# Moving the on-the-way weight sums of the second layer's output projection from pairs 2 and 3 to pairs 4 and 5, with side work in every second step

## The chip, the cores and the metric

The kernel runs on one core of a Trainium2 chip. The metric is the device time of one execution in microseconds (us). The time before is the median of three runs, 2347.38 us (2345.62 to 2347.71).

## The reference, cut to what matters

One inference step of a two-layer decoder over 1024 prompt tokens and 8 decode tokens, width 2048. Layer A is a pooling mixer, layer B is windowed attention with a gate. Both end in an output projection, a residual and a layer norm. The change touches the output projection of layer B alone:

```python
def attn_layer(x, pos, kb, vb, k_pos, q_pos, blocked, w_in, sinks, w_out, g_ln, b_ln):
    ...
    o = attn_core(q, kb, vb, q_pos, k_pos, sinks).reshape(B, T, D_ATTN)
    y = (o * jax.nn.silu(gate)) @ w_out
    return layer_norm(ALPHA * x + y, g_ln, b_ln)
```

## The kernel before

**Phases.** The tokens are cut into two chunks, chunk 0 with 512 columns and chunk 1 with 520. The phases run one after the other: `ai` (input projection and pooling of layer A), `ao` (its output projection), `bi` (input projection and attention of layer B), `bo` (its output projection). "bo, chunk 0" is the second output projection's first chunk. It follows "bi, chunk 1", and "bo, chunk 1" follows it and ends the kernel.

**Strassen products.** A product of 2048 by 2048 weights is worked in eight pairs of output tiles, here pair 0 to pair 7. Each pair is one 2x2 block product by a seven-product scheme. The four weight blocks of a pair are a11, a12, a21 and a22, each 128 x 1024 fp32 (512 KB). Three of the seven products use a block as it stands (indices 0, 5 and 6: a11, a12, a22). Four use sums of blocks (indices 1 to 4). In f32r every product is made from a high part and a low part, so one product is three matmuls for each of eight slices of K: lines 655, 656 and 657 (high x high, high x low, low weight x high), 24 matmuls in all.

**Steps.** One such product is a step. Bo, chunk 0 has 56 steps, counted here from 0. Pairs 0 and 1 are interleaved in steps 0 to 13 (`both`). Pair p from 2 on has steps 7p to 7p + 6 in the order of indices 0, 2, 1, 5, 3, 4, 6 (`ORDER7`). So pair 2 has steps 14 to 20, pair 3 steps 21 to 27, pair 4 steps 28 to 34, pair 5 steps 35 to 41.

**What a step issues.** `begin` first flushes the evictions of the step before (`posts`: lines 594, 600, 603, 609, 615, 628 on ACT, lines 616 and 621 on DVE, and after a pair's last product line 1234, the residual, on DVE). Then it loads weights, casts them to their high part (line 476, ACT), takes the low part (line 491, DVE), and makes sums. How far ahead each is done stands in `self.ahead`, (a, b, d): at step e weights are loaded up to step e + a - 1, cast up to e + b - 1, and their low part is taken up to e + d - 1. Sums are made up to e + b. From the last pair of bi on, `ahead` is (6, 3, 2). From the end of step 23 of bo, chunk 0 it is (7, 4, 3). The first of the three matmuls that needs the low part is line 657, the third matmul of a step.

**Where the sums come from.** There are two ways. `next_pair` loads all seven blocks ready made, the four sums from the scratch tensor `swob`, into which `sum_gen` has put them during bi (lines 425 to 430). `first_pair` loads the four blocks (a22 twice, five loads), makes the sums on the way with four additions on DVE (line 334), uses them, and stores them to `swob` (line 335, a DMA issued from POOL), since chunk 1 needs them again. `LATE` names the pairs of `wob` that go by `first_pair` in bo, chunk 0. `sum_gen` leaves these out.

**Other work in bo, chunk 0.** After each pair come line 1277 (subtract the shift), 1283 (square, ACT), 1288 and 1289 (two running sums), all 128 x 1024, and a store (line 1279, POOL). In steps 0 to about 20 the last of the attention and the decode tokens' attention still run (lines 1759 to 1979). From step 18 on there is side work, the generator `t_gen` for the activations "o" of chunk 1: a load (line 836, SP), four subtractions and additions of 128 x 260 on DVE (lines 823 to 826) and a store (line 827, POOL), eight times. It advances by one item in `end`, at most once in `self.every` steps:

```python
        if self.side and int(self.i / self.every) != int((self.i - 1) / self.every) and room >= self.room:
            if next(self.side[0], 1):
                self.side.pop(0)
```

`every` is 3 for a phase that does not set it, so also for bo, chunk 0. What is left is done at once when the next phase's inputs are first wanted (`x_begin`, between steps 41 and 42). From there on the activations of chunk 1 are loaded, cast (line 766) and split (line 775) beside the weights.

**Order.** PE, DVE and ACT each run in the order of the source (`in_order`), so an instruction that waits holds all behind it. SP issues the loads and POOL most stores, each in an order that the scheduler sets from the readiness of the buffers. All large tiles share 53 slots (`Mem`).

Of the kernel before, what the change touches and what calls it, by code (L numbers as in the profile page):

```python
# [69 lines left out]
    (7, 3), (7, 4), (5, 5), (5, 6), (6, 5), (6, 6), (7, 5), (7, 6),  # L70
)

LATE = (2, 3)
X_KEEP = 5
X_AGE = 3
SIDE_KEEP = 5
# [106 lines left out]
class Kern:  # L183
# [177 lines left out]
    def build_stream(self):  # L361
        io = self.io
        w = []
        for kind, c, part in PHASES:
# [20 lines left out]
            else:  # L385
                name = "woa" if kind == "ao" else "wob"
                if (kind, c, part) != PHASES[-1]:
                    prs = [self.next_pair(name, q) for q in range(8)]
                    if (kind, c) == ("bo", 0):
                        for q in LATE:  # L390
                            prs[q] = self.first_pair(name, q)
# [10 lines left out]
    def sum_gen(self, name):  # L402


        W = 256
        qs = [q for q in range(8) if name != "wob" or q not in LATE]
        parts = [(q, slice(W * h, W * h + W)) for q in qs for h in range(4)]
# [144 lines left out]
    def both(self, c, P, Q):  # L552

        runs = [self.seven(c, z0, z1, {6: done}, own=own) for (z0, z1, done), own in (
            (P, self.psW), (Q, self.psW if self.wide else self.psO)
        )]
        for idx in ORDERL:
            for run in runs:
                run(idx)

    def pair(self, c, z0, z1, done, c11=None):

        run = self.seven(c, z0, z1, {6: done}, c11)
        for idx in ORDER7:
            run(idx)
# [1535 lines left out]
    def run(self):  # L2101
        io = self.io
        self.build_stream()
        self.needs, self.pe, self.summed, self.hurry = [], {}, {}, None
        self.sg, self.qs, self.ao = {}, {}, {}
        self.last = self.turn = self.lock = False
        self.need = {}
        self.shared = False
        self.strassen = False
        self.start()  # L2110

        def add(key, gen):
            self.needs.append((key, gen))
            self.side.append(gen)

        acc, before = {}, False
        for n, (kind, c, part) in enumerate(PHASES):
            self.c, self.ph = c, kind + str(c)
            self.strassen = (kind, c, part) not in PLAIN
            self.shared = False  # L2120
            self.fresh = c == 1 and before and self.strassen
            before = c == 0 and self.strassen
            nxt = n + 1 if n + 1 < len(PHASES) else None
            self.every, self.room = 3, SIDE_KEEP
            if n == 0 or (kind, c) == ("bi", 0) and self.wide:
                self.use_four(kind == "ai")
            elif (kind, c) == ("bo", 0):
                self.at(18, lambda: self.use_four(True))

            self.lock = (kind, c) in LOCKED  # L2130
            self.need = {
                (idx, g): self.i + (2 * n + g - 1 if self.lock else n)
                for n, idx in enumerate(ORDERL if self.lock else ORDER7) for g in range(2)
            } if self.strassen else {}
            self.turn = not self.lock
            self.at(7, lambda: setattr(self, "turn", False))
            self.at(13, lambda: setattr(self, "lock", False))
            if n == 0:
                pass
            elif (kind, c) == ("ai", 0):  # L2140
                add(("x", 1, False), self.t_gen(("x", 1)))
                self.room = 99
            elif (kind, c) == ("ai", 1):
                add(("g", 0, False), self.t_gen(("g", 0)))
                self.summed["woa"] = 0
                add("woa", self.sum_gen("woa"))
                self.every = 1.7
            elif (kind, c) == ("ao", 0):
                self.every = 2
            elif (kind, c) == ("ao", 1):  # L2150
                gen = self.ln_gen(0, *acc[0], C_GA, C_BA, self.act["h", 0], None)
                self.at(3, lambda gen=gen: add(("h", 0, True), gen))
                self.every = 2
            elif (kind, c) == ("bi", 0) and not self.strassen:
                self.summed["wob"] = 0
                self.extra = self.sum_gen("wob")
                for k in (4, 24):
                    self.at(k, lambda k=k: setattr(self, "on", k == 4))
                add(("h", 1, False), self.ln_gen(1, *acc[1], C_GA, C_BA, self.act["h", 1], self.Td.get(("h", 1))))
                add(("h", 0, False), self.t_gen(("h", 0)))  # L2160

                for k in range(10):
                    self.at(2 * k + 3, lambda: self.side and self.lastO < self.i - 1 and self.side_step())
                self.every = 1.2
            elif (kind, c) == ("bi", 1):
                self.at(8, lambda: setattr(self, "on", True))
                self.every, self.room = 1, 0
            elif (kind, c) == ("bo", 0):
                self.at(23, lambda: setattr(self, "ahead", (7, 4, 3)))
                self.at(18, lambda: add(("o", 1, False), self.t_gen(("o", 1))))  # L2170
                self.at(16, lambda: [s.free() for s in self.kv])
                self.rt.free()
            elif (kind, c) == ("bo", 1):
                gen = self.ln_gen(0, *acc[0], C_GB, C_BB, io["y0"], None)
                self.at(3, lambda gen=gen: add("y", gen))
                self.every = 3
            if kind == "ai":
                self.phase_ai(c, range(*part), nxt)
            elif kind == "bi":
                self.phase_bi(c, range(*part), nxt)  # L2180
            else:
                res = self.act["x" if kind == "ao" else "h", c]
                last = (C_GB, C_BB, io["y1"]) if nxt is None else None
                acc[c] = self.phase_out(c, res, nxt, last)
# [146 lines left out]
```

## Time and profile before

| | us |
|---|---|
| median of three runs | 2347.38 |
| the profiled execution, whole | 2344.57 |
| its span, first to last instruction | 2342.8 |

The profiled execution is 2.81 us under the median. What lies around its span is 1.77 us. In the lines shown below, a row of a timeline has start, duration, engine, line, operation and operands, and in square brackets the idle time before it and what ended it. A row of a list of groups has count, busy time and mean. A row of the windows has the busy time of PE, PE's weight loads, DVE, ACT and POOL in that stretch, then the granted clock, the share of the DMA engines and GB/s. Times in a timeline count from the start of the span.

### The profile page before, as it was taken

What the parts mean: (1) busy time and instruction counts of PE and PEld (TensorE: products, weight loads), DVE (VectorE), ACT (ScalarE), POOL (GpSimd) and SP (SyncE); (2) the same over time, 40 slices, a digit from 0 to 9 for tenths busy, and PEclk for the clock granted to TensorE, in tenths of its full rate; (3) what the DMA queues carried; (4) which work ended last, traced back from release to release, by engine and by line L of the source; (5) the groups of instructions that cost most, each with busy time, mean ns of one, the idle gap of its engine ahead of it and who ended that gap; (6) DMA issues with size and microseconds to landing.
All of it is one profiled execution on the core that took longest, in us unless ns stands there. A gap on an engine that the chain in (4) does not pass through costs nothing. (4 is left out here: it accounts for less than half of the span.)

```text
span 2342.8 us, 49652 instructions
## 1 busy us (share of the span) xinstructions
PE 2302.7 (98%) x19960; PEld 2202.7 (94%) x19960; DVE 1923.7 (82%) x2386; ACT 1365.4 (58%) x2502; POOL 202.3 (9%) x379
## 2 busy tenths in 40 slices
PE   8999999999999999999999999999999999999997
PEld 6899999999999999998777899999999999999997
DVE  8788988777878878868998898897777778889887
ACT  4454446544546557655464666685666668556656
POOL 0111110010000000000111111100000000000000
PEclk9999999999999999999999999999999999999999
DMA  8668789989889989999799766788776768699785
GB/s 293 213 242 310 272 287 343 328 290 326 299 302 328 323 286 329 320 339 325 262 330 360 254 235 225 253 297 279 249 249 231 231 199 299 230 355 371 268 303 196
DMA packets 252072, 669.39 MB, mean 286 GB/s; under 512 B 25760, under 2 KB 106560, under 8 KB 251840
## 3 DMA queue, kind: packets, MB, share of 16 engines
q1 hardware_dynamic: 206368, 501.14, 63.3%
q0 software_dynamic: 45472, 165.07, 18.2%
q8 instruction: 156, 2.56, 0.4%
q14 instruction: 76, 0.62, 0.1%
HBM read 471.01 MB, written 185.59 MB: 280 GB/s over the span
## 5 line engine op out<-in xcount | busy, mean ns | idle before, releaser
L655 PE MATMUL pD<-m,m 128*128 128x260 f32 (+1 forms) x4752 | 1346.2, 283 | 4.7 <-ACT pD L594 2.8
L657 PE MATMUL pD<-m,m 128*128 128x260 f32 (+1 forms) x4752 | 1340.3, 282 | 6.2 <-DVE m L491 6.1
L656 PE MATMUL pD<-m,m 128*128 128x260 f32 (+1 forms) x4752 | 1339.8, 282 | 1.1 <-DVE m L775 1.1
L491 DVE TENSOR_TENSOR m<-m,m 128x1024 fp32r<-128x1024 f32 x674 | 814.2, 1219 | 114.8 <-ACT m L476 59.7
L655 PEld LDWEIGHTS pD<-m,m 128*128 128x128 f32 x4752 | 895.5, 188 | 13.2 <-issue 5.1
L657 PEld LDWEIGHTS pD<-m,m 128*128 128x128 f32 x4752 | 895.9, 189 | 8.5 <-DVE m L491 8.5
L656 PEld LDWEIGHTS pD<-m,m 128*128 128x128 f32 x4752 | 895.5, 188 | 1.8 <-DVE m L775 1.3
L476 ACT CAST m<-m 128x1024 fp32r<-128x1024 f32 x674 | 703.4, 1049 | 251.5 <-DVE m L334 69.6
L683 PE MATMUL pD<-m,m 128*128 128x512 f32 x448 | 179.5, 401 | 8.1 <-ACT m L766 8.1
L684 PE MATMUL pD<-m,m 128*128 128x512 f32 x448 | 177.2, 395 | 1.0 <-DVE m L775 1.0
L685 PE MATMUL pD<-m,m 128*128 128x512 f32 x448 | 177.0, 395 | 0.0
L775 DVE TENSOR_TENSOR m<-m,m 128x1024 fp32r<-128x1024 f32 (+1 forms) x120 | 146.9, 1225 | 6.9 <-ACT m L766 5.4
L766 ACT CAST m<-m 128x1024 fp32r<-128x1024 f32 (+1 forms) x120 | 125.8, 1052 | 14.1 <-PE pD L684 5.2
L683 PEld LDWEIGHTS pD<-m,m 128*128 128x128 f32 x448 | 84.6, 189 | 29.5 <-ACT m L766 8.1
L334 DVE TENSOR_TENSOR m<-m,m 128x1024 f32<-128x1024 f32 x88 | 107.6, 1222 | 4.3 <-DMA m<-in_wia 2.6
L684 PEld LDWEIGHTS pD<-m,m 128*128 128x128 f32 x448 | 84.6, 189 | 20.8 <-DVE m L775 2.1
L685 PEld LDWEIGHTS pD<-m,m 128*128 128x128 f32 x448 | 84.5, 189 | 19.7
L616 DVE TENSOR_TENSOR m<-pD,m 128x260 f32<-128x260 f32 (+1 forms) x86 | 36.0, 419 | 80.6 <-ACT pD L615 73.8
L628 ACT COPY m<-pD 128x260 f32<-128x260 f32 (+1 forms) x83 | 31.0, 374 | 117.9 <-PE pD L657 117.8
L1795 ACT ACTIVATE m<-m,sm 128x128 f32<-128x128 f32 x256 | 99.2, 391 | 0.0
L1085 PE MATMUL pD<-m,m 128*128 128x260 f32 (+1 forms) x528 | 91.5, 323 | 0.0
L1808 ACT ACTIVATE m<-m,sm 128x128 f32<-128x128 f32 x256 | 81.9, 392 | 12.8 <-DVE sm L1803 12.8
(245 smaller groups left out, 2113.1 us busy)
## 6 DMA issues: line engine op xcount, KB each, us to landing
m<-in_wia SPq DMA_DIRECT2D x124, 512.0 KB
m<-in_wib SPq DMA_DIRECT2D x120, 512.0 KB
swia<-m POOLq DMA_DIRECT2D x64, 512.0 KB, 4.8
m<-swia SPq DMA_DIRECT2D x64, 512.0 KB
m<-swoa SPq DMA_DIRECT2D x64, 512.0 KB
swib<-m POOLq DMA_DIRECT2D x64, 512.0 KB, 5.4
m<-swib SPq DMA_DIRECT2D x64, 512.0 KB
m<-swob SPq DMA_DIRECT2D x56, 512.0 KB
```

What stands on the lines that cost most here:

```text
L334: self.nc.vector.tensor_add(s[out].a[:, :1024], s[x].a[:, :1024], s[y].a[:, :1024])
L476: self.nc.scalar.copy(hi.r[:, :1024], self.stream[self.cast].src().a[:, :1024])
L491: self.nc.vector.tensor_sub(lo.r[:, :1024], s.src().a[:, :1024], hi.a[:, :1024])
L655: nc.tensor.matmul(ps[:, :TH], wh[:, s], h, start=new and k == 0, stop=False, skip_group_check=on)
L656: nc.tensor.matmul(ps[:, :TH], wh[:, s], l, start=False, stop=False, skip_group_check=on)
L657: nc.tensor.matmul(ps[:, :TH], wl[:, s], h, start=False, stop=k == 7, skip_group_check=on)
L683: nc.tensor.matmul(ps[:], wh[:, s], h, start=par == 0 and k == 0, stop=False)
L684: nc.tensor.matmul(ps[:], wh[:, s], l, start=False, stop=False)
L685: nc.tensor.matmul(ps[:], wl[:, s], h, start=False, stop=par == 1 and k == 7)
L766: self.nc.scalar.copy(h.r[:, :n], s.a[:, :n])
L775: self.nc.vector.tensor_sub(l.r[:, :n], s.a[:, :n], h.a[:, :n])
L1795: nc.scalar.activation(x["s3"][:, i, :], x["s3"][:, i, :], AF.Exp, bias=nm[:, i : i + 1], scale=0.125, accum_out=rs[:, i : i + 1],)
```

## The change

`LATE` names pairs 4 and 5 in place of pairs 2 and 3, and the phase bo, chunk 0 advances its side work every second step in place of every third.

```diff
-LATE = (2, 3)
+LATE = (4, 5)
@@ run
             elif (kind, c) == ("bo", 0):
+                self.every = 2
                 self.at(23, lambda: setattr(self, "ahead", (7, 4, 3)))
                 self.at(18, lambda: add(("o", 1, False), self.t_gen(("o", 1))))
```

Both programs have the same number of instructions on PE, DVE, ACT and POOL. `sum_gen` makes the sums of pairs 0, 1, 2, 3, 6 and 7 during bi in place of 0, 1, 4, 5, 6 and 7. On DVE the eight additions of line 334 and the eight groups of lines 823 to 826 stand elsewhere. On POOL and SP the stores and loads that belong to them move along.

## The prediction

> **What bounds the kernel now.** I read the page's first part, then PE's waits, then the timelines of PE, DVE and ACT over bo, chunk 0.
>
> ```profile
> PE 2302.7 (98%) x19960; PEld 2202.7 (94%) x19960; DVE 1923.7 (82%) x2386; ACT 1365.4 (58%) x2502; POOL 202.3 (9%) x379
> ```
>
> PE is busy 2302.7 of 2342.8 us, so everything the change can win is in PE's idle time, and what it can lose is new idle time. The change reaches only bo, chunk 0 and what follows. PE's waits between 2010 and 2060 us, the steps in which pairs 2 and 3 make their sums, are these (total, times, longest):
>
> ```profile
> PE pD L657 <- DVE m L491: 2.5, 4, 1.4
> PE pS L1836 <- DVE m L1822: 0.7, 1, 0.7
> ```
>
> All five wait for DVE, four for the low part of a weight. Those that matter here, with the start of step 21 (2047.82) and of step 22 (2050.61), and one in the next activations' stage:
>
> ```profile
> 2025.77 1.97 PE L1836 MATMUL pS<-m,m 128*64 128x128 f32 x32 [0.70 <-DVE m L1822]
> ...
> 2028.64 0.39 PE L657 MATMUL pD<-m,m 128*128 128x256 f32 x1 [0.47 <-DVE m L491]
> ...
> 2047.82 0.28 PE L655 MATMUL pD<-m,m 128*128 128x256 f32 x1
> ...
> 2050.61 0.28 PE L655 MATMUL pD<-m,m 128*128 128x256 f32 x1
> 2050.73 0.28 PE L656 MATMUL pD<-m,m 128*128 128x256 f32 x1
> 2052.39 0.38 PE L657 MATMUL pD<-m,m 128*128 128x256 f32 x1 [1.38 <-DVE m L491]
> ...
> 2144.21 0.38 PE L657 MATMUL pD<-m,m 128*128 128x256 f32 x1 [0.74 <-DVE m L491]
> ```
>
> The first two matmuls of a step start 0.12 us apart, so the third of step 22 was due at 2050.85 and came at 2052.39: the step lost 1.54 us where the row shows 1.38 of idle time. I add 0.16 to each wait for this restart. Between 2053 and 2143 us PE has no wait at all. That is the stretch into which the change moves DVE's work.
>
> **Part 1: the sums of pairs 2 and 3 go.** DVE around these waits:
>
> ```profile
> 2022.10 2.48 DVE L334 TENSOR_TENSOR m<-m,m 128x1024 f32<-128x1024 f32 x2
> 2024.50 1.22 DVE L1822 TENSOR_TENSOR m<-pS,cst 128x1024 f32<-128x1024 f32 x1
> ...
> 2047.59 2.48 DVE L334 TENSOR_TENSOR m<-m,m 128x1024 f32<-128x1024 f32 x2
> 2049.98 1.22 DVE L1234 SCALAR_TENSOR_TENSOR m<-m,m 128x1024 f32<-128x1024 f32 x1
> 2051.12 1.22 DVE L491 TENSOR_TENSOR m<-m,m 128x1024 fp32r<-128x1024 f32 x1
> 2052.26 1.22 DVE L1277 TENSOR_TENSOR m<-m,m 128x1024 f32<-128x1024 f32 x1
> ```
>
> From start to start a wide instruction (128 x 1024) holds DVE 1.14 us. Two additions stand straight ahead of L1822, without which it starts 2.4 us sooner, and 0.70 disappears. So does the 0.47 behind it, whose L491 follows L1822 without a break. The two at 2047.59 hold L1234, and behind it the L491 for which step 22 waits. Without them L1234 starts when its copy on ACT (L628) is done, 0.6 us into step 21, and that L491 is done at 0.6 + 1.14 + 1.22 = 2.96 us, where it is due at 2.79 + 0.24 = 3.03. So the 1.38 disappears, by a hair. The gain is 0.70 + 0.47 + 1.38 + 3 x 0.16 = 3.0 us. The other two L657 waits, 2.5 - 0.47 - 1.38 = 0.65 us, I leave: both follow decode work that waits for PE itself. Bounds: 2.2 (the restarts and half of the last wait stay) to 3.7.
>
> **Part 2: DVE in steps 21 to 40 after the change.** Two successive L628, seven steps apart, give the step's length, (2089.38 - 2069.51) / 7 = 2.838 us:
>
> ```profile
> 2069.51 0.37 ACT L628 COPY m<-pD 128x256 f32<-128x256 f32 x1 [1.82 <-PE pD L657]
> ...
> 2089.38 0.37 ACT L628 COPY m<-pD 128x256 f32<-128x256 f32 x1 [3.36 <-PE pD L657]
> ```
>
> What DVE does between 2047.8 and 2101 us now, by groups, and one side-work item (L823 to the next instruction, 1.49 us):
>
> ```profile
> L491 DVE TENSOR_TENSOR m<-m,m 128x1024 fp32r<-128x1024 f32 x19 | 22.7, 1218 | 0.0
> L1234 DVE SCALAR_TENSOR_TENSOR m<-m,m 128x1024 f32<-128x1024 f32 x3 | 3.7, 1222 | 2.7 <-ACT m L628 2.7
> L334 DVE TENSOR_TENSOR m<-m,m 128x1024 f32<-128x1024 f32 x3 | 3.7, 1222 | 0.1
> ...
> L823 DVE TENSOR_TENSOR m<-m 128x260 f32<-128x260 f32 x5 | 2.1, 425 | 0.0
> ```
>
> ```profile
> 2065.85 0.43 DVE L823 TENSOR_TENSOR m<-m 128x260 f32<-128x260 f32 x1
> ...
> 2067.34 0.42 DVE L621 TENSOR_TENSOR m<-pD,m 128x256 f32<-128x256 f32 x1
> ```
>
> In the changed program's order the instructions from the L1234 of step 21 to the L491 issued in step 38 are 19 L491, 12 others of a pair's end (L1234, L1277, L1288, L1289 three times), 8 L334 (steps 25, 26, 26, 29 for pair 4, steps 32, 33, 33, 36 for pair 5), 4 short ones (L616, L621; 0.34 each), and all 8 side-work items (ends of steps 23, 25, ... 37). That is 39 x 1.14 + 4 x 0.34 + 8 x 1.49 = 44.5 + 1.4 + 11.9 = 57.8 us. The first cannot start before 0.6 us into step 21, so the last ends 58.4 us into it. It makes the low part for step 40 (`ahead` is 3 by then), which is due 19 steps and 0.24 us in: 19 x 2.838 + 0.24 = 54.2. DVE is never without work between, so PE loses 58.4 - 54.2 = **4.2 us** there, in pieces ahead of steps 33, 36, 38 and 40: 0.3, 2, 0.3 and 1.5 by the same tally. Before, the same stretch has 34 wide ones (19 + 3 x 4 + 3) and 5 items, 34 x 1.14 + 1.4 + 5 x 1.49 = 47.6 us, some 6 less than the steps last, and DVE's idle time in the rows above (2.7 us at L1234) shows it. Bounds: 3.2 (1.12 for a wide one) to 5.0 (1.16); and ACT, whose casts of the sums wait for L334 with the evictions queued behind them, is busy only 30.5 of 60 us here (the first windows row below), which I cost at nothing (one cast, 1.05 us, if that cover is gone).
>
> **Part 3: transfers.** The moved additions carry their DMAs: pairs 4 and 5 each issue five loads and four stores in place of seven loads, pairs 2 and 3 the reverse, and the side work's stores come sooner. Rows of the transfers issued between 2040 and 2100 us, and of two windows:
>
> ```profile
> to<-m POOLq DMA_DIRECT2D x4, 520.0 KB, 7.1
> swob<-m POOLq DMA_DIRECT2D x4, 512.0 KB, 6.5
> ```
>
> ```profile
> 2040.00:2100.00 60.00, 58.44 (x492) 58.03 (x491) 53.68 (x63) 30.54 (x42) 5.88 (x11) 1.00 0.98 356
> ...
> 2120.00:2130.00 10.00, 10.00 (x86) 9.99 (x85) 6.06 (x7) 4.65 (x6) 0.00 (x0) 1.00 1.05 402
> ```
>
> Here four more swob stores, about three more to-stores and about two fewer weight loads make 5 or 6 transfers of 0.52 MB more, 21.4 + 2.9 = 24.3 MB. In 60 us that is 405 GB/s, and in the 64 us that the stretch then lasts, 380. The later window moved 402, so I cost it at nothing beside DVE's own delay: 3 steps lie between load and cast. [...] The trace shows 402 in a window, so I go by the trace; what the 356 row would mean as a ceiling is the second rival.
>
> **Part 4: after step 41.** Before, three side-work items are left and run at once there, their three stores go into the queue together with the new activations' loads, and later a weight lands late:
>
> ```profile
> 2130.18 1.05 ACT L476 CAST m<-m 128x1024 fp32r<-128x1024 f32 x1 [1.76 <-DMA m<-swob]
> 2131.13 0.37 ACT L628 COPY m<-pD 128x256 f32<-128x256 f32 x1
> ```
>
> The third matmul at 2144.21 was due 0.9 earlier, so its step 54 began at 2143.07 and step 49 five steps before, at 2128.9. L628 comes some 0.2 us into a step, but stood behind that cast until 2131.13: DVE's chain (L1234 and all behind it) began 2 us late, and the wait of 0.74 followed. Without the three stores (3 x 0.52 MB at 402 GB/s = 3.9 us) the cast is not late. Gain 0.74 + 0.16 = 0.9 us; bounds 0 to 1.2. POOL's stores pass each other without holding an engine, and one swob load that SP now issues already in bi is one transfer, 1.3 us of a queue, at nothing.
>
> **Sum.** 4.2 - 3.0 - 0.9 = +0.3 us; I round to **+0.5** for the two leads that hold by a hair (0.07 us in step 22). On the profiled execution that is 2344.57 + 0.5 = 2345.1; carried to the median of the runs, which is 2.81 higher, **2347.9 us**. A relief in one place is given back in the next.
>
> **The rivals.**
> *The overload is absorbed.* If DVE's lag in steps 24 to 40 costs PE nothing, only the gains stay: -3.9 us, 2343.5. For it: two steps of lead from step 24 on, and no wait at all in the stretch before. Against it: the work is 4.2 us more than that lead holds, with the lead already counted in.
> *Slower: the DMA queue becomes the bound.* If 356 GB/s is what this mix of transfers gets, the stretch needs 24.3 / 0.356 = 68 us in place of 60: 8 us late. DVE's additions wait for blocks loaded one or two steps before, and all L491 behind them. The stretch then costs 8 in place of 4.2, and the 0.9 of part 4 doesn't come: 8 - 3.0 = +5.0, 2352.4. It decides once landing times, 6.5 to 7.1 us in the rows above, pass some 11. For it: a share of 0.98 at 356. Against it: 402 at 1.05. [...]
> *The side work does not advance.* It needs five free slots. The program order shows it taken in each second step, so this is out.
>
> **How the numbers follow.** About 0.2% (4.7 us) is what a measurement of this kernel can tell from no change. The likeliest, DVE gives back what it gained, has 0.65: bounds -1.7 (3.2 - 3.7 - 1.2) to +2.8 (5.0 - 2.2), 2345.7 to 2350.2. The absorbed overload has 0.13 and is mostly within 0.2% too. The DMA bound has 0.17, about two thirds of it over 0.2%, and 0.05 is left for what I don't see. So faster 0.06, same 0.80, slower 0.14. The range takes in both rivals: 2343.2 to 2353.5.
>
> **What would show it.** Right: PE's waits at L1836 and at step 22 gone; new L657 waits for L491 ahead of steps 33 to 40, some 4 us together; DVE without idle time from step 21 to 38; the cast near 2130 not waiting for a DMA. Wrong: no PE wait in steps 24 to 41 (the overload is absorbed), or L334 and L491 there waiting for a DMA (the queue bounds). A new wait in bi, or a change of the last 150 us, would make the prediction wrong in a place it doesn't look at.

## The result, and the profile after

The changed kernel takes 2351.67 us (median of 12 runs, 2348.78 to 2352.76), the kernel before, run beside it, 2347.09. The ratio is 1.0018, with a 95% interval from 1.0010 to 1.0026: that is some 4.2 us slower (2.3 to 6.1). The profiled execution takes 2350.97 us, its span is 2349.2. The first line of its page:

```profile
PE 2305.3 (98%) x19960; PEld 2205.1 (94%) x19960; DVE 1923.1 (82%) x2386; ACT 1365.7 (58%) x2502; POOL 202.3 (9%) x379
```

The engines have the same instructions as before. Of the 6.4 us by which the span is longer, PE's busy time has 2.6 and its idle time 3.8.

Three stretches between the same matmuls in both traces show where the time went. They are bounded by a matmul that waits 0.52 us in both traces, by the third matmul of step 22, by the third matmul of step 40, and by one in bo, chunk 1. The rows of before (timeline of PE; the second, 2052.39, stands in the prediction):

```profile
2022.24 0.39 PE L657 MATMUL pD<-m,m 128*128 128x256 f32 x1 [0.52 <-DVE m L491]
...
2103.63 0.28 PE L657 MATMUL pD<-m,m 128*128 128x256 f32 x1
...
2195.59 0.28 PE L656 MATMUL pD<-m,m 128*128 128x260 f32 x1
```

The same four matmuls after, with the two other long waits of PE:

```profile
2024.00 0.39 PE L657 MATMUL pD<-m,m 128*128 128x256 f32 x1 [0.52 <-DVE m L491]
...
2051.12 0.37 PE L657 MATMUL pD<-m,m 128*128 128x256 f32 x1
...
2082.80 0.39 PE L655 MATMUL pD<-m,m 128*128 128x256 f32 x1 [3.40 <-ACT m L603]
...
2098.12 0.39 PE L657 MATMUL pD<-m,m 128*128 128x256 f32 x1 [1.99 <-DVE m L491]
...
2111.43 0.39 PE L657 MATMUL pD<-m,m 128*128 128x256 f32 x1 [1.03 <-DVE m L491]
...
2201.69 0.28 PE L656 MATMUL pD<-m,m 128*128 128x260 f32 x1
```

| stretch | before | after | difference | forecast |
|---|---|---|---|---|
| early: to step 22 | 30.15 | 27.12 | -3.03 | -3.0 |
| middle: step 22 to step 40 | 51.24 | 60.31 | +9.07 | +4.2 |
| late: from step 40 on | 91.96 | 90.26 | -1.70 | -0.9 |
| sum | | | +4.34 | +0.3 |

The sum agrees with the 4.2 us that the ratio gives. Another 1.8 us of the longer span lie ahead of the first of these matmuls (2024.00 against 2022.24). In the kernels below that do the same work up to there, it starts between 2021.65 and 2029.80, so this is scatter between executions.

The early gain is the forecast one. The middle costs more than twice what was forecast. The wait at 2082.80 is of another kind than those forecast: PE waits for an eviction on ACT (L603), ahead of the first matmul of step 32. ACT's timeline there, and the store on POOL that it waits for:

```profile
2075.52 0.35 ACT L600 COPY m<-pD 128x256 f32<-128x256 f32 x1
2081.43 1.04 ACT L476 CAST m<-m 128x1024 fp32r<-128x1024 f32 x1 [5.56 <-DMA to<-m]
2082.38 0.36 ACT L603 COPY m<-pD 128x256 f32<-128x256 f32 x1
```

```profile
2071.46 0.53 POOL L827 DMA_DIRECT2D to<-m  x1 [2.42 <-DVE m L826]
```

The cast's input came earlier; what it waits for last is a slot. Its new tile takes the slot of a side-work item whose store was issued at 2071.46 and lands ten microseconds later. L603, which empties the accumulator that PE wants next, is queued behind it. The wait at 2098.12 follows another of this kind: DVE's low part stood still for a store of the side work as well.

```profile
2088.89 1.23 DVE L491 TENSOR_TENSOR m<-m,m 128x1024 fp32r<-128x1024 f32 x1 [3.68 <-DMA to<-m]
```

The windows from 2064 to 2090 us show how full the DMA queue is, first before, then after (columns as in the front part; the last two are the share of the DMA engines and GB/s):

```profile
2064.00:2090.00 26.00, 26.00 (x223) 26.00 (x221) 21.11 (x30) 12.71 (x19) 2.13 (x4) 1.00 0.95 340
```

```profile
2064.00:2090.00 26.00, 22.60 (x179) 22.40 (x178) 21.48 (x29) 8.95 (x13) 4.27 (x8) 0.93 1.01 400
```

The stores that POOL issued in that window after, with the median us from issue to landing:

```profile
to<-m POOLq DMA_DIRECT2D x4, 520.0 KB, 9.5
swob<-m POOLq DMA_DIRECT2D x3, 512.0 KB, 9.1
```

Before, the two took 7.1 and 6.5 from 2040 to 2100 us (the prediction's rows); after, over those 60 us, 8.9 and 7.7. The queue moves 400 GB/s in this window, a rate that the forecast took as free, but its stores take longer to land. By the trace's records of issue and landing, one weight load (issued 2074.07, landed 2088.57) took 14.5 us.

### The profile page after: what moved, and what is told of

It reads as the page before. It is cut to its first block, busy times and chain, and to the rows that moved or that the text cites. A ratio compares the mean times of both kernels' runs of the same rounds, so it can differ in the third digit from the quotient of the medians.

```text
span 2349.2 us, 49653 instructions
## 1 busy us (share of the span) xinstructions
PE 2305.3 (98%) x19960; PEld 2205.1 (94%) x19960; DVE 1923.1 (82%) x2386; ACT 1365.7 (58%) x2502; POOL 202.3 (9%) x379
```

## The experiments

Three theories. *Work*: DVE has more to do in steps 21 to 38 than its lead holds, as forecast. *Slot*: a tile freed by a side-work item is given to a cast or a low part while its store is still under way. *Queue*, also called bytes: the DMA queue is full, and whatever transfer is late then holds ACT or DVE. Beside each median ratio stand the three stretches, as in the table above (early, middle, late), from the one profiled execution of each kernel.

**One part of the change alone.** First the moved pairs without the quicker side work:

```diff
             elif (kind, c) == ("bo", 0):
-                self.every = 2
```

> Half of the change: pairs 4 and 5 make their sums on the way, side work stays at every third step. Theory 'work' (DVE has more work between steps 21 and 40 than time): 39 wide instructions, 4 short ones and 5 items are 53.4 us from 0.6 us into step 21, against 54.2, so PE loses nothing there, the 3.0 us of early relief stay, the burst of three items at step 42 stays too: about 2344 us. Theory 'slot' (a cast or a low part is written into the slot of a side-work item whose store is still under way, and holds its engine until the store lands): the stores of pairs 4 and 5 still fill the queue, and slots are still reused after 11 to 17 new tiles, so some wait for a to-store remains: 2346 to 2349 us.

Ratio 1.0009 (1.0000 to 1.0018); stretches -3.01, +1.95, +4.08. The loss is there without the quicker side work, so the moved pairs bring it, with their additions, loads and stores. Work alone expected none. Most of it comes later, ahead of step 41, where an eviction on ACT waits for a store of the side work and PE for ACT:

```profile
2107.81 0.37 ACT L609 COPY m<-pD 128x256 f32<-128x256 f32 x1 [5.82 <-DMA to<-m]
```

```profile
2109.45 0.58 PE L655 MATMUL pD<-m,m 128*128 128x256 f32 x1 [2.31 <-ACT pD L615]
```

Then the quicker side work with the old pairs:

```diff
-LATE = (4, 5)
+LATE = (2, 3)
```

> The other half: pairs 2 and 3 as before, side work every second step. Theory 'work': 34 wide ones, 4 short ones and 8 items are 52.1 us against 54.2 from step 21 to 40, so no new wait, the early waits stay, and the burst at step 42 and the 0.9 us behind it go: about 2346 us. Theory 'slot': without the eight sum stores in the same stretch a to-store lands in some 7 us, before its slot is wanted: the same 2346 us. If the faster side work alone were the cost: 2350 us or more.

Ratio 0.9994 (0.9985 to 1.0003); stretches 0.00, +0.88, -2.08. The early waits stay, and the late gain comes with the quicker side work alone. The +0.88 of the middle, a new wait of 0.76 us for a low part in step 25, was not expected.

**Take the slot wait away.** In the order in which slots are given on, the slot of a side-work item comes 14 releases later than before (24 in place of 10), to keep it from being taken while its store is under way:

```diff
         nc.gpsimd.dma_start(dst[:, kp], t)
-        s.free(True)
+        s.mem.release(s, 24 if self.ph == "bo0" else 10)
```

> The changed kernel, with the slot of a side-work item in this phase coming free 14 releases later in the order of slots (24 in place of 10), so that it is taken again 20 to 31 new tiles later in place of 11 to 19. No instruction more or less. Theory 'slot': the cast that waited 5.6 us and the low part that waited 3.7 us for a to-store wait no more, PE's stall of 3.4 us and the half clock behind it (1.5 us) go: about 2346.5 us, with some 3 to 4 us of waits for the low part left. Theory 'work': DVE's queue is as long as before, PE's loss stays: 2351 us.

Ratio 1.0017 (1.0008 to 1.0025); stretches -3.03, +8.11, -1.92. No instruction of ACT or DVE waits for a to-store any more, and the loss is nearly the same. Now DVE waits for a block of a weight, and its lag comes out at PE in several smaller waits:

```profile
2089.69 1.23 DVE L334 TENSOR_TENSOR m<-m,m 128x1024 f32<-128x1024 f32 x1 [3.59 <-DMA m<-in_wob]
...
2097.78 0.38 PE L657 MATMUL pD<-m,m 128*128 128x256 f32 x1 [2.25 <-DVE m L491]
```

Slot as the only cause falls: the wait changes its place. ACT waits 2.4 us for such a block too.

**Take DVE's work away.** In bo, chunk 0 the four additions of a side-work item give way to one memset on POOL; load and store stay, the stored values are zeros:

```diff
-        nc.vector.tensor_sub(t[:, 1, :], E[:, a], E[:, b])
...
+        if self.ph == "bo0":
+            nc.gpsimd.memset(s.a[:, : 4 * TH], 0.0)
```

> The changed kernel, with the four additions of each side-work item in this phase left out: POOL fills the item's tile with zeros in their place, and the load and the store stay. Theory 'work': DVE has 11.9 us less to do, no wait for the low part is left between steps 24 and 41: about 2344 us. Theory 'slot': loads, stores and slots are as in the changed kernel, so the cast still waits for the to-store, and the stall of 3.4 us and the half clock stay: about 2348 to 2349 us.

Ratio 0.9988 (0.9979 to 0.9997); stretches -3.06, +4.85, -1.78. With 11.9 us less on DVE the middle loses 4.2 us less than in the changed kernel, but not nothing. What is left is one wait behind a late block, and a granted clock of one half for 3.41 us behind it, in which the same matmuls fall back by another 1.5 us (the last section has more on this):

```profile
2086.63 1.23 DVE L334 TENSOR_TENSOR m<-m,m 128x1024 f32<-128x1024 f32 x1 [6.88 <-DMA m<-in_wob]
...
2089.37 0.39 PE L657 MATMUL pD<-m,m 128*128 128x256 f32 x1 [3.26 <-DVE m L491]
```

```profile
2090.84:2094.25 3.41, 3.41 (x18) 3.41 (x18) 3.41 (x4) 2.45 (x4) 1.87 (x4) 0.50 1.02 413
```

The ratio is 2.8 us of gain where this execution's stretches sum to 0.0, so other executions may lose less there.

**Take the transfers away, and both.** The first kernel issues neither the swob stores of pairs 4 and 5 nor the to-stores of the side work; chunk 1 reads other stored tensors of the same size. The second also leaves the side work's additions out.

```diff
-                self.nc.gpsimd.dma_start(ws[:, i, :], s[out].a[:, :1024])
+                if name != "wob":
+                    self.nc.gpsimd.dma_start(ws[:, i, :], s[out].a[:, :1024])
...
-        nc.gpsimd.dma_start(dst[:, kp], t)
+        if dst is not self.Td["o", 1]:
+            nc.gpsimd.dma_start(dst[:, kp], t)
```

> The changed kernel without 16 stores in bo, chunk 0: the eight of the sums of pairs 4 and 5 (swob) and the eight of the side work (to). Chunk 1 loads other stored tensors of the same size in their place, so its transfers stay, and its output differs. All additions on DVE stay where they are, 8.3 MB of transfers go. Theory work (DVE has 4.2 us more to do than its lead holds): the waits of PE for the low part in steps 33 to 40 stay, some 4 us together, without any DMA behind them; with the gains of the early steps (-3.0) and of part 4 (-0.9 to -1.8) the time is 2346.5 to 2347.7. Theory queue (DVE and ACT are held by transfers that land 10 to 14 us after issue, the additions alone would fit): landing times fall below 8 us, no wait of PE over 1 us and no half clock is left, 2342.5 to 2344.

Ratio 1.0006 (0.9997 to 1.0015); stretches -3.04, +4.63, -1.62. This is the answer on DVE's work: from step 21 to step 40 no wait for a DMA is left on ACT or DVE, DVE has no pause, and PE loses 4.6 us where 4.2 were forecast. The window (DVE busy 25.69 of 26 us, 269 GB/s), then PE's waits from 2060 to 2120 us, then the two longest of them in its timeline (lines are one higher in this kernel, L492 is the low part):

```profile
2064.00:2090.00 26.00, 25.63 (x215) 25.21 (x215) 25.69 (x36) 11.20 (x16) 0.54 (x1) 1.00 0.80 269
```

```profile
PE pD L658 <- DVE m L492: 3.2, 3, 1.6
```

```profile
2099.47 0.39 PE L658 MATMUL pD<-m,m 128*128 128x256 f32 x1 [1.58 <-DVE m L492]
...
2112.78 0.39 PE L658 MATMUL pD<-m,m 128*128 128x256 f32 x1 [1.34 <-DVE m L492]
```

> As the run without the 16 stores, and also without the 32 additions of the side work on DVE (8 x 1.49 = 11.9 us); the loads stay, the output differs. Both theories: only the gains are left, -3.0 and -0.9 to -1.8, 2342.5 to 2343.8. A wait of PE over 1 us in steps 24 to 41 would be a third cause that neither names. Theory work says it is 3 to 4 us below the run without the stores alone, theory queue says the two agree within 1 us.

Ratio 0.9985 (0.9976 to 0.9994); stretches -3.03, -0.19, -2.04. With both gone the middle costs nothing, so no third cause is left. The four middles nearly add up: side work's additions without the stores +4.6, stores without these additions +4.9, both +9.1, neither -0.2. The ratios agree less well. Against the ratio of neither (0.9985), the additions cost 4.9 us, both 7.7, but the stores without the additions only 0.7, each with an uncertainty of some 3 us. How much the stores cost in other executions stays open; in the one profiled, 1.5 of the 4.9 is the halved clock.

**Which stores.** One kind left out at a time, by the one or the other edit of the kernel without stores.

> The changed kernel without the eight swob stores of pairs 4 and 5 (4.2 MB); chunk 1 loads other pairs' sums in their place, so the output differs. With all 16 stores gone PE lost 4.6 us in steps 24 to 41 where the changed kernel lost 9.1; the other 4.5 are to be placed. Theory slots (the side work's stores hold the tiles that ACT and DVE want): this run stays at 8 to 9 us lost there, ratio to before 1.0015 to 1.002. Theory bytes (what counts is how full the queue is, whichever store fills it): landing times fall to 6 to 9 us, 4.6 to 6 us lost, no half clock, ratio 1.0005 to 1.001.

Ratio 1.0004 (0.9995 to 1.0013); stretches -3.04, +5.66, -1.70.

> The changed kernel without the side work's eight stores (4.3 MB); chunk 1 loads another stored tensor of the same size, so the output differs. Theory slots: no wait for a side work store can be left, so all of the 4.5 us go, 4.6 us lost in steps 24 to 41 as without all 16, ratio 1.0005. Theory bytes: about the same as the run without the swob stores, 4.6 to 6 us lost, ratio 1.0005 to 1.001. The two kinds together tell: slots says they differ by 4 us, bytes says by less than 1.5.

Ratio 1.0005 (0.9996 to 1.0013); stretches -3.02, +4.63, -1.69. The two middles differ by 1.0 us, as bytes expected, which allowed 1.5. In the first, ACT still waits for a to-store, but 2.9 us in place of 5.6, which fits the 1.0 us that it loses more. Its wait, its window, and the window of the kernel without to-stores:

```profile
ACT m L477 <- DMA to<-m: 2.9, 1, 2.9
```

```profile
2064.00:2090.00 26.00, 25.00 (x208) 24.49 (x208) 24.76 (x34) 10.48 (x15) 2.13 (x4) 1.00 0.92 342
```

```profile
2064.00:2090.00 26.00, 25.63 (x213) 25.03 (x212) 25.69 (x36) 10.92 (x15) 3.20 (x6) 1.00 0.95 360
```

At 342 and 360 GB/s in that window the transfers cost 1.0 and 0.0 us beyond DVE's 4.6, at the changed kernel's 400 they cost 4.4. The three kernels with fewer stores have ratios of 1.0004 to 1.0006, the two with all stores and all work (the changed one and that with the late slots) 1.0018 and 1.0017. No pair of intervals is apart, but the five fall into two groups.

**Versions that might beat both.** Four complete kernels. Two with other pairs, `LATE = (2, 5)` and `LATE = (5, 6)`:

> The changed kernel with pairs 2 and 5 on the way in place of 4 and 5. The early waits of 0.70 and 0.47 stay, the 1.38 goes (pair 3 makes no sums). Theory work: DVE's tally for steps 21 to 38 falls by pair 4's four additions, 57.8 - 4.6 = 53.2 us, under the 54.2 that the lead holds, so nothing is lost there: -1.5 - 1.2 = 2344.4 to 2345.2. Theory queue: pair 4 now loads seven blocks in place of five loads and four stores, only 1 MB of 24 less, so landing times stay over 10 us and a wait of 2 to 4 us stays: 2346 to 2348.5.

Ratio 0.9998 (0.9989 to 1.0006); stretches -1.54, +2.06, -1.90.

> The changed kernel with pairs 5 and 6 on the way in place of 4 and 5: no sums in steps 14 to 28, those of pair 6 in steps 39 to 43, when the side work has ended. Theory work: 53.2 us of DVE's work in a lead of 54.2, nothing lost up to step 40, so -3.0 and -0.9: 2343.3 to 2344.5, unless the splits of chunk 1's activations after step 41 collide with pair 6's sums. Theory queue: 1 MB less up to step 36, landing times over 10 us stay, 2345.5 to 2348.

Ratio 0.9997 (0.9988 to 1.0006); stretches -3.04, +3.64, -1.56. Here theory work missed: both tallies are 1 us under the lead, and both lose 2 to 4 us. DVE waits 1.1 and 2.7 us for late transfers in them, and in the first ACT 3.2 us. A spare of 1 us can't hold that; how much of the loss is DVE's own was not separated. In the first, the window from 2064 to 2090 us has nearly the changed kernel's rate, and PE is never idle in it:

```profile
2064.00:2090.00 26.00, 26.00 (x222) 26.00 (x221) 23.68 (x34) 11.29 (x17) 3.74 (x7) 1.00 0.99 385
```

One with the side work earlier, `self.every = 1` in place of 2:

> The changed kernel with side work in every step from step 18 on: three or four items and their stores come before step 21 and all end by step 27, ahead of pair 4's and 5's sums. Theory overload in a lead: DVE's tally for steps 21 to 38 is 57.8 less 3 or 4 items of 1.49 us, 52 to 53.4, under the 54.2 of the lead, and the stores of the side work no longer meet those of the sums: less than 2 us lost in steps 24 to 41, 2343 to 2344.5. Rival: five more items (7.5 us of DVE) in steps 18 to 27, where casts run only two or three steps ahead, make new waits of 2 to 4 us there: 2346 to 2348.

Ratio 1.0023 (1.0014 to 1.0033); stretches -3.02, +10.68, -1.88. Both forecasts missed; the rival, which expected new waits, was nearer. The long waits on ACT and DVE are for stores of the side work again. That these come closer together and their tiles are wanted sooner would explain it, but is not shown.

```profile
ACT m L476 <- DMA to<-m: 4.6, 1, 4.6
...
DVE m L491 <- DMA to<-m: 4.1, 1, 4.1
```

One with the side work's additions on POOL:

```diff
+        ve = nc.gpsimd if dst is self.Td["o", 1] else nc.vector
-        nc.vector.tensor_sub(t[:, 1, :], E[:, a], E[:, b])
+        ve.tensor_sub(t[:, 1, :], E[:, a], E[:, b])
```

> The changed kernel with the side work's subtractions and additions in bo, chunk 0 on POOL in place of DVE; the output is complete. Theory work and queue: DVE's tally falls by 11.9 to 45.9 us, no overload is left, and the full queue costs what it cost when the additions were left out, one wait of about 3 us and a half clock: 2344 to 2345.5. Rival: the four operations take POOL several us per item, and the stores of sums and results queued behind them go out late and hold the tiles longer: a stall of more than 4 us, 2346 to 2350.

Ratio 1.0076 (1.0063 to 1.0089); stretches -3.07, +20.31, -0.26. The row of one of the four groups on POOL (busy, mean ns) gives 1.36 us for what DVE does in 0.42. An item takes 5.3 us there, the sum of the four groups' means, and the loss is larger than the rival said. What PE waits for in it is not shown.

```profile
L826 POOL TENSOR_TENSOR m<-m,m 128x260 f32<-128x260 f32 x8 | 10.9, 1361 | 0.0
```

None of the complete versions is shown to be faster than the kernel before. The nearest is the quicker side work with the old pairs, and its interval (0.9985 to 1.0003) reaches past 1. Loading the blocks further ahead was not tried.

## Why the prediction was right, and where it was wrong

The forecast was +0.5 us and 2347.9, mostly within 0.2%; the ratio is 1.0018. The direction and the range hold, but the range does so only because it takes in the rivals: the measured +4.2 lies outside the bounds of the likeliest case (-1.7 to +2.8), and nearest to the rival of the DMA queue (+5.0), which had a chance of 0.17. Two of those bounds don't come out of their own terms. Part 1's lower one is 1.9 where 2.2 is written (0.70 + 0.47 + half of 1.38), part 2's is 3.4 where 3.2 is written (39 wide ones at 1.12); with them the likeliest case reaches from -1.5 to +3.1, and still falls short. By its steps:

- *Part 1, -3.0*: -3.03 measured, and the same within 0.04 in every kernel that moves both pairs. The lead of 0.07 us in step 22 held.
- *Part 2, +4.2 from DVE's work*: shown by the kernel without stores, +4.63, with DVE never idle from step 21 to step 40. Differences between the same matmuls there and before give the pieces: 0.3 in step 32, 0.6 in step 33, 0.3 at the start of step 34, 1.9 in step 36, 0.3 in step 38, 1.5 in step 40, with 0.2 the other way in small differences between, for a forecast of 0.3, 2, 0.3 and 1.5 in steps 33, 36, 38 and 40. The rival that the overload is absorbed falls with this.
- *Part 3, transfers at nothing*: this is the step that failed, and with it the sentence of part 2 that costs ACT at nothing. The size of the traffic was nearly right. The matmuls that run from 2040 to 2100 us before take 66.1 us after, in which the queue moves 357 GB/s, 23.6 MB against a forecast of 24.3. But it does not come evenly, at the 380 to 405 GB/s of the forecast: it is 400 for 26 us and less around them. The error was to read a rate that the queue can move as a rate that is free. At that rate a store of the side work took 9.5 us in place of 7.1. The prediction counted only the three steps between a load and its cast, not the new tile that waits for a store's slot. Price: 9.07 - 4.63 = 4.4 us in the traces, and 1.0018 against 1.0006 in the ratios, 2.8 us with intervals that overlap. The windows above give no single rate from which transfers cost: 342 cost 1.0 us by one late store, 360 nothing, and at 385 PE was never idle in the window. What counted in them was which transfer was late and what stood behind it.
- *The rival of the queue* had the mechanism: late transfers hold DVE's additions and low parts. Its condition was landing times of 11 us; a store of 10 was enough. Its price was the bytes over 356 GB/s, 8 us in place of 4.2. The stretch did cost 9.1, and moved no more than 357 GB/s over its 66.1 us, so the number came close. But 356 is not what the queue can give at most: from 2040 to 2100 us the kernel without the side work's additions, which issues the same transfers, moved 376. What the traces show are waits for single transfers beside DVE's overload, not a longer transfer of all bytes.
- *Part 4, -0.9*: -1.7. The wait of 0.74 is gone as forecast. Two smaller ones behind it went as well, which the forecast left standing. The list of PE's waits from 2120 to 2240 us had three before and is empty after:

```profile
PE pD L657 <- DVE m L491: 1.0, 2, 0.7
PE pD L655 <- ACT m L609: 0.5, 1, 0.5
```

Without the stores the three stretches sum to -0.03 us, for a forecast of +0.3: what was counted came out right in sum (part 2 was 0.4 too low, part 4's gain 0.7), and what was left out made the difference. What stays open is how the 4.4 us fall on other executions of the changed kernel. Which transfer is late, and what it holds, differs from kernel to kernel in the traces, and only one execution of each was profiled.

## What to carry to other kernels

A transfer rate seen in some window (402 GB/s here) shows that the queue moved so much, not that it is free: at 400 a store of the side work took 9.5 us to land in place of 7.1. When a change brings a stretch near it, cost the longer landing time against every tile whose slot is given on while its store is under way, and name what stands behind that instruction in its engine's queue. A tally of an in-order engine's work against its lead gave the size and place of a loss to some tenths of a microsecond here (4.2 us forecast, 4.63 without the stores), as long as nothing from outside delayed the engine. A wait that one edit removed in a full queue came back at another transfer: taking bytes out helped (a middle of 5.66 or 4.63 us in place of 9.07), moving the wait did not (8.11).

## What the runs showed of the hardware

The stall at 2082.80 cost more than its 3.4 us. Two windows of the changed kernel, the end of the stall and the time behind it (the granted clock is the figure after POOL's): the granted clock is 0.50 for 3.41 us, and 1.00 again from 2087.68 to 2091.09.

```profile
2080.86:2084.27 3.41, 1.47 (x12) 1.48 (x13) 2.85 (x4) 2.54 (x4) 0.00 (x0) 1.00 1.02 418
2084.27:2087.68 3.41, 3.41 (x18) 3.41 (x18) 0.91 (x3) 1.41 (x2) 0.53 (x1) 0.50 1.03 420
```

The trace has 18 matmuls there where the next kernel's row shows 31, and the same matmuls fall behind by another 1.5 us. That is a third of the 4.4, as far as it would not have been lost in DVE's later waits without it; this was not separated. The kernel whose slots are given back late has a stall of 2.25 us and keeps its clock at 1.00:

```profile
2095.96:2099.37 3.41, 1.59 (x13) 1.59 (x14) 3.41 (x5) 2.40 (x4) 0.53 (x1) 1.00 0.87 356
2099.37:2102.78 3.41, 3.41 (x31) 3.41 (x31) 3.38 (x7) 1.32 (x2) 0.53 (x1) 1.00 0.51 154
```

In the run of the moved pairs alone a stall of 2.31 us was followed by a clock of 0.50 as well:

```profile
2105.69:2109.10 3.41, 1.46 (x13) 1.25 (x11) 1.14 (x2) 1.29 (x3) 0.53 (x1) 1.00 1.03 419
2109.10:2112.51 3.41, 3.06 (x14) 3.06 (x15) 3.08 (x5) 2.21 (x4) 0.00 (x0) 0.50 1.00 389
```

PE stood idle for 1.94 us in the first of the changed kernel's two windows and for 1.95 in the first of these, and for 1.82 in the first of the kernel with the late slots. What decides whether the clock is halved is not shown by these few windows.
